# The last down-projection group's late weight tiles, and who scales, squares and sums in the final norm

## The chip, the cores and the metric

The kernel runs on one core of a Trainium2 chip. That core has five engines, each with its own instruction stream: TensorE (PE, the matmuls), VectorE (DVE), ScalarE (ACT), GpSimd (POOL) and SyncE (SP, which here only issues DMAs). They meet through semaphores. Weights and activations come from the chip's main memory by DMA into SBUF; TensorE writes its results into PSUM, from where VectorE and ScalarE evict them. The metric is the device time of one execution in microseconds (us), of which the median of a few runs counts.

## The reference

One layer of a streaming encoder for a prompt of 1024 tokens and a sample of 64: a mixer of retention and sliding-window attention, cross-attention, and a gated feed-forward part, each behind an RMS norm and added to the residual; then a final RMS norm. The change is in the last two lines of this:

```python
def rms_norm(x, g=None):
    xf = x.astype(jnp.float32)
    y = xf * lax.rsqrt(jnp.mean(xf * xf, axis=-1, keepdims=True) + EPS)
    if g is not None:
        y = y * g.astype(jnp.float32)
    return y.astype(x.dtype)

def swiglu(x, g_ffn, w_gate, w_up, w_down):
    hn = rms_norm(x, g_ffn)
    return (jax.nn.silu(hn @ w_gate) * (hn @ w_up)) @ w_down

hp = hp + swiglu(hp, g_ffn[l], w_gate[l], w_up[l], w_down[l])
...
y_prompt = rms_norm(hp, g_final)
```

The model width is 1024 and the feed-forward width 2816; everything is float32.

## The kernel before, in words

Activations are held transposed: 128 features on the partitions, 1088 tokens (prompt and sample, `T`) along the free dimension. The residual before the final norm is eight such tiles, `y[0]` to `y[7]` (`KT` = 8). In the trace and in the lists below `y[0]` goes by the name `rstd_f`, `y[1]` and `y[2]` share a tile, `y[3]` and `y[4]` another, and `y[5]`, `y[6]`, `y[7]` are tiles of their own.

Each float32 matmul is made of three: every operand is split into a high part (ScalarE's cast, L124) and a low part (VectorE's subtraction, L125), and high x high, high x low and low x high are summed in PSUM (L157 to L159 in `mm3`, L223 to L226 in `multiply`). Large products go by Strassen's scheme with seven products P1 to P7, whose weight operands are sums of raw weight tiles. In the last stages GpSimd forms these sums (L201, L202, L204, L207 in `weight_ops`).

`down` multiplies by `w_down` in three groups of the 22 blocks of 128 along the feed-forward width (8, 8 and 6). In each group the eight output rows come in pairs `m`. For each pair two raw weight tiles are loaded into a pool `wp` with two buffers for them (`raw`), split, multiplied and added to `y` (L1646, L1648). In the last group (`last`) the products P2 and P4 are left out, and `complete` squares the right half of the tokens (columns 544 to 1087, which hold the sample) as soon as its rows are done (ScalarE) and adds the squares up in `rstd` (VectorE, L1660). After that, a loop over the same row pairs loads what P2 and P4 need once more, 128x768 at a time into the same two buffers, splits it into `wb`, and hands it to `finish` in `rest`: sixteen late products of nine matmuls, for each of two quarters of the tokens (columns 0 to 271, then 272 to 543) and each of the eight rows.

`finish` runs the final norm beside these late products. It has three column ranges: 0 and 1 are the two quarters, 2 is the right half. For each range: `grow` adds the product to `y` (VectorE) and squares it (ScalarE), `gather` adds the square to `rstd` (VectorE), `sums` adds over the partitions by a matmul with ones, `roots` takes the inverse root in five small steps of VectorE and one of ScalarE, `spread` brings the roots back to all partitions by a matmul with the identity, and ScalarE copies them to `rstd` where `copied` is set. Then each row is multiplied by gain and root and stored. `scale` does it in one VectorE instruction and issues the store; `gain` (ScalarE) and `aside` (GpSimd, then the store) do it in two.

A scheduler lays out the order of each engine's instructions from the program's dependencies and its own estimates, and `queued` and `in_order` pin VectorE's and TensorE's order in `finish`. `issue_after` holds an instruction's place behind another's. Each engine then runs its list strictly in order. PSUM banks come from a pool of four pairs, taken in turn, and a product can begin only when the pair's former contents have been evicted. All loads and nearly all stores are issued by SyncE, in order.

Of the kernel before, what the change touches and what calls it, by code (L numbers as in the profile page):

```python
# [19 lines left out]
P = 128  # L20
# [89 lines left out]
class Kernel:  # L110
# [1525 lines left out]
    def down(self, starts):  # L1636
# [28 lines left out]
        for gi, g in enumerate(GROUPS):  # L1665
            last = gi == len(GROUPS) - 1
            f0, n = starts[gi], g * P // 2
            for m in range(0, KT, 2):
# [5 lines left out]
                raws = [self.wp.tile([P, 1024], F32, tag="raw", bufs=2, name="raw") for i in range(2)]  # L1674
                with self.tc.issue_after(self.loaded) if m == 2 and not last else nullcontext():
                    for i in range(2):
                        load_half(raws[i][:, :2 * n], m + i, f0, f0 + g)
                if m == KT - 4 and not last:
                    for name in ("B11", "B21" if gi == 0 else "T2"):
                        self.ahead[name, gi + 1] = list(self.fetch(name, gi + 1))  # L1680
# [10 lines left out]
                else:  # L1691
# [5 lines left out]
                    if m == 0:  # L1697
                        for name in ("B21", "T4"):
                            self.load_operand(name, gi)
                if last and m == KT - 4:  # L1700
                    nc.scalar.activation(self.root[:, 0, :1], self.rstd[:, HALF:HALF + 1], AF.Sqrt)
        rest = []
        for m in range(0, KT, 2):
            raw = self.wp.tile([P, 1024], F32, tag="raw", bufs=2, name="raw")
            for i in range(2):
                load_half(raw[:, i * n:(i + 1) * n], m + i, f0 + g // 2, f0 + g)
            ring, slots = self.slots["B11" if m < 4 else "T1"]
            q = self.rings[ring].tile("wb", slot=slots[m // 2 % 2])
            self.last_queued = self.split(raw[:, :2 * n], q[:, 0, :2 * n], q[:, 1, :2 * n])
            rest += [(m + i, q[:, :, i * n:(i + 1) * n], self.ops[("B21", "T4")[i]]) for i in range(2)]  # L1710
# [7 lines left out]
    def finish(self, y, rest):  # L1718
# [29 lines left out]
        def sums(c, *more):  # L1748
# [4 lines left out]
            for i, (a, w) in enumerate(spans):  # L1753
                for j, x in enumerate(parts):
                    self.last_mm = nc.tensor.matmul(ps[:, i, :], x[:, a:a + w], self.ones[:, :2], start=j == 0,
                                                    stop=j == len(parts) - 1).ins
# [9 lines left out]
        def spread(c, copied=True):  # L1766
            r, spans, _ = factors[c]
            for part in ((0, 2), (2, 5)) if len(spans) > 4 else ((0, len(spans)),):
# [7 lines left out]
                if copied:  # L1776
                    nc.scalar.copy(self.rstd[:, c0 + a0:c0 + a1], pb[:, :a1 - a0])
# [12 lines left out]
        def aside(c, k, queue=nc.sync):  # L1790
            o = y[k][:, cols[c]]
            nc.gpsimd.tensor_tensor(out=o, in0=o, in1=self.rstd[:, cols[c]], op=ALU.mult)
            queue.dma_start(self.io["o_y"][k, :, cols[c]], o)

        for j in range(2 * KT):
# [3 lines left out]
            if (j - 1) % KT and j:  # L1799
# [9 lines left out]
            if j == KT + 6:  # L1809
                pb0 = self.in_order(lambda: spread(0, False))[:, :HC]  # L1810
            if c and m < KT - 1:
                scale(2, m)
            if c and KT - 5 < m < KT - 1:
                gain(1, rest[m][0])
            if j == 2 * KT - 2:
                gain(2, KT - 1)
                aside(2, KT - 1)
        m = rest[-1][0]
        spare = [rest[i][0] for i in range(KT - 4, KT - 1)]
        scale(0, 0, pb0)  # L1820
        scale(0, 1, pb0)
        self.in_order(lambda: sums(1, squares[1, m]))
        roots(1, lambda: scale(0, 2, pb0))
        for k in range(3, KT):
            scale(0, k, pb0)
        pb = self.in_order(lambda: spread(1))[:, :HC]
        queues = [nc.sync, nc.scalar]
        rows = [k for k in range(KT) if k not in spare]
        for i, k in zip((2, 4, 7), spare):
            rows.insert(i, k)  # L1830
        for i, k in enumerate(rows):
# [86 lines left out]
```

## Time and profile before

| what | us |
| --- | --- |
| median of three runs | 2156.85 |
| lowest and highest of them | 2153.68, 2157.04 |
| profiled execution, its own time | 2156.32 |
| its span, first to last instruction | 2154.5 |
| TensorE busy in the span | 2133.1 |
| VectorE, ScalarE, GpSimd busy | 1550.4, 875.0, 531.9 |

The rows of the profile that the prediction shows are of four kinds. A row of a timeline gives start, duration, engine, line, operation, output and inputs, form and count, and in brackets how long the engine had been idle and what ended that. A row of waits gives total, number and longest. A row of stretches gives length, then busy time of each engine with its number of instructions, the clock granted to TensorE as a share of full, the share in which the 16 DMA engines were busy, and GB/s; where one engine alone was asked for, it is shorter. SPq and ACTq are the DMA issues of SyncE and ScalarE.

### The profile page before, as it was taken

To read this page: it belongs to the slowest core of one execution; us is meant where nothing else is said; L and a number is where in the kernel's file an instruction comes from. 1 tells how busy PE (TensorE), PEld (TensorE's weight loads), DVE (VectorE), ACT (ScalarE), POOL (GpSimd) and SP (SyncE) were. 2 spreads that over 40 slices of the span, in tenths; PEclk is the share of its full clock that TensorE was granted. 3 is DMA by queue.
4 is the path that set the end of the run, shared out by engine and by line. 5 is a ranking of instruction groups with operands and counts; after the bars stand their busy time and mean duration, and the time that the engine had idled before them with its cause. 6 is when DMAs were issued, how large, how long until landed. Compare 5 with 4: busy or idle time off the path is not lost.

```text
span 2154.5 us, 41702 instructions
## 1 busy us (share of the span) xinstructions
PE 2133.1 (99%) x16371; PEld 2082.9 (97%) x16371; DVE 1550.4 (72%) x2912; ACT 875.0 (41%) x1894; POOL 531.9 (25%) x448
## 2 busy tenths in 40 slices
PE   9999999999999999999999999999999999999997
PEld 9999999999999997889999999999999999999997
DVE  8987969776677567656545555678777777878597
ACT  8344434344434356553233343343223222344243
POOL 0000000022243125540000000015555555523531
PEclk9999999999999999999999999999999999999998
DMA  7334444434345485336443121413342232384333
GB/s 267 122 127 123 131 140 135 127 118 160 111 143 191 155 257 189 115 115 210 144 133 103 43 72 53 147 61 103 126 148 86 101 126 93 125 306 161 105 116 113
DMA packets 169893, 290.85 MB, mean 135 GB/s; under 512 B 39266, under 2 KB 96546, under 8 KB 169698
## 3 DMA queue, kind: packets, MB, share of 16 engines
q1 hardware_dynamic: 161666, 269.02, 38.8%
q0 software_dynamic: 3424, 10.82, 1.4%
q10 hardware_dynamic: 4608, 8.36, 1.0%
q8 instruction: 129, 2.11, 0.4%
q14 instruction: 66, 0.54, 0.1%
HBM read 196.97 MB, written 91.16 MB: 134 GB/s over the span
## 4 chain that ended last, share of the span: by engine, by line
PE 88%; DVE 5%; issue 2%; DMA 2%; ACT 2%; POOL 1%; SPq 0%; POOLq 0%; DVEq 0%; ACTq 0%
PE pq L226 18%; PE pq L223 17%; PE pq L224 17%; PE pd L157 8%; PE pd L158 8%; PE pd L159 8%; DVE wq L125 1%; PE pout L1078 1%; PE pss L1008 1%; PE pk L769 1%; DVE T L125 1%; PE pp L1054 1%; PE po L158 1%; PE po L159 1%; PE po L157 1%
## 5 line engine op out<-in xcount | busy, mean ns | idle before, releaser
L124 ACT CAST wq<-raw 128x512 fp32r<-128x512 f32 (+1 forms) x499 | 302.2, 614 | 560.8 <-PE pq L226 233.1
L125 DVE TENSOR_TENSOR wq<-raw,wq 128x512 fp32r<-128x512 f32 (+1 forms) x499 | 427.0, 860 | 131.9 <-ACT wq L124 128.5
L224 PE MATMUL pq<-T,wq 128*128 128x272 f32 x1832 | 492.1, 288 | 0.0
L223 PE MATMUL pq<-T,wq 128*128 128x272 f32 x1832 | 490.3, 287 | 1.4 <-ACT wq L124 0.6
L224 PE MATMUL pq<-B,wq 128*128 128x272 f32 x1592 | 426.8, 288 | 0.0
L223 PE MATMUL pq<-B,wq 128*128 128x272 f32 x1592 | 425.4, 287 | 0.0
L226 PE MATMUL pq<-T,wq 128*128 128x272 f32 x1832 | 382.7, 289 | 1.9 <-DVE wq L125 1.9
L201 POOL TENSOR_TENSOR raw<-raw 128x512 f32<-128x512 f32 (+1 forms) x44 | 64.0, 1454 | 1254.2 <-DVE wq L125 536.8
L223 PEld LDWEIGHTS pq<-T,wq 128*128 128x128 f32 x1832 | 344.3, 188 | 2.7 <-issue 1.1
L224 PEld LDWEIGHTS pq<-T,wq 128*128 128x128 f32 x1832 | 344.0, 188 | 1.0 <-issue 0.7
L226 PE MATMUL pq<-B,wq 128*128 128x272 f32 x1592 | 332.0, 289 | 0.0
L224 PEld LDWEIGHTS pq<-B,wq 128*128 128x128 f32 x1592 | 299.0, 188 | 0.5 <-issue 0.4
L223 PEld LDWEIGHTS pq<-B,wq 128*128 128x128 f32 x1592 | 298.9, 188 | 0.1
L226 PEld LDWEIGHTS pq<-T,wq 128*128 128x128 f32 x1832 | 289.6, 189 | 3.6 <-DVE wq L125 2.4
L226 PEld LDWEIGHTS pq<-B,wq 128*128 128x128 f32 x1592 | 251.7, 189 | 0.9 <-issue 0.7
L277 DVE TENSOR_TENSOR u<-pq,u 128x544 f32<-128x544 f32 x177 | 127.5, 721 | 82.4 <-PE pq L226 82.2
L616 DVE TENSOR_TENSOR stage<-pq,u 128x544 f32<-128x544 f32 x112 | 80.4, 720 | 30.3 <-PE pq L226 25.5
L157 PE MATMUL pd<-xc,wq 128*128 128x256 f32 (+1 forms) x256 | 74.6, 292 | 0.0
L159 PE MATMUL pd<-xc,wq 128*128 128x256 f32 (+1 forms) x256 | 74.3, 290 | 0.0
L158 PE MATMUL pd<-xc,wq 128*128 128x256 f32 (+1 forms) x256 | 74.1, 290 | 0.0
L1566 POOL TENSOR_TENSOR stage<-stage,rstd_f 128x544 f32<-128x544 f32 x40 | 63.8, 1605 | 39.1 <-ACT stage L1565 39.1
L204 POOL TENSOR_TENSOR raw<-raw 128x512 f32<-128x512 f32 (+1 forms) x44 | 58.9, 1339 | 51.5 <-DVE wq L125 49.0
(388 smaller groups left out, 4517.4 us busy)
## 6 DMA issues: line engine op xcount, KB each, us to landing
hl<-d_op SPq DMA_DIRECT2D x85, 272.0 KB, 5.1
d_qkv<-stage SPq DMA_DIRECT2D x44, 272.0 KB, 2.3
d_op<-stage SPq DMA_DIRECT2D x44, 272.0 KB, 2.2
d_op<-ht SPq DMA_DIRECT2D x44, 272.0 KB, 3.6
raw<-w_gate SPq DMA_DIRECT2D x22, 512.0 KB, 3.6
raw<-w_up SPq DMA_DIRECT2D x22, 512.0 KB, 5.0
raw<-w_down SPq DMA_DIRECT2D x16, 512.0 KB, 4.9
d_gate<-stage ACTq DMA_DIRECT2D x28, 272.0 KB, 2.9
```

Source lines behind the costliest of these rows:

```text
L124: self.last_cast = self.nc.scalar.copy(hi, src).ins
L125: return self.nc.vector.tensor_tensor(out=lo, in0=src, in1=hi.bitcast(F32), op=ALU.subtract).ins
L157: mm(ps, wh, xh, start=start, stop=False)
L158: mm(ps, wh, xl, start=False, stop=False)
L159: self.last_mm = mm(ps, wl, xh, start=False, stop=stop).ins
L201: tt(out=a11, in0=a11, in1=a21, op=sub)
L223: mm(ps[:, c, :HC], w[:, 0, ks], x[:, 0, cs], start=start, stop=False)
L224: mm(ps[:, c, :HC], w[:, 0, ks], x[:, 1, cs], start=False, stop=False)
L226: self.last_mm = mm(ps[:, c, :HC], w[:, 1, ks], x[:, 0, c * HC:(c + 1) * HC], start=False, stop=stop).ins
L277: add = lambda out, a, b: nc.vector.tensor_tensor(out=out, in0=a, in1=b, op=ALU.add)
L616: nc.vector.tensor_tensor(out=o, in0=ps, in1=sb, op=ALU.add)
L1566: nc.gpsimd.tensor_tensor(out=g, in0=g, in1=r[t], op=ALU.mult)
```

## The change

The diff has three parts.

First, the weights. Once the last group's first row pair has been sent off, the six extra buffers of another pool (`self.temp`) are given up, and a pool of four tiles of 128x768 is opened in their place (`raw_tile`). The last row pair's two raw tiles come from it, and so do the first two of the four late tiles (`halves`); the other two still come from `wp`. All of them are issued behind the last operand load (`self.loaded`), ahead of the last row pair's products. Second, `sums` orders its matmuls by operand rather than by token block, with one start flag for all, and the last two squares of quarter 1 go into it as operands of their own instead of being added up by VectorE first. Third, the scalings are dealt out anew: rows 5, 6 and 7 of the right half go to ScalarE's gain and GpSimd's `aside`, as does row 7 of quarter 0, for which the first quarter's roots are now copied to SBUF; of quarter 1, rows 5 and 6 go that way, no longer 4, 5 and 6.

```diff
--- before.py
+++ after.py
@@ -1671,10 +1671,17 @@
                     if last and t == 1:
                         complete(m + i, HALF, HALF)
 
-                raws = [self.wp.tile([P, 1024], F32, tag="raw", bufs=2, name="raw") for i in range(2)]
-                with self.tc.issue_after(self.loaded) if m == 2 and not last else nullcontext():
+                raws = [self.raw_tile() if last and m == KT - 2 else self.wp.tile([P, 1024], F32, tag="raw", bufs=2, name="raw")
+                        for i in range(2)]
+                with self.tc.issue_after(self.loaded) if m == (KT - 2 if last else 2) else nullcontext():
                     for i in range(2):
                         load_half(raws[i][:, :2 * n], m + i, f0, f0 + g)
+                if m == KT - 2 and last:
+                    halves = [self.raw_tile() for k in range(2)]
+                    halves += [self.wp.tile([P, 1024], F32, tag="raw", bufs=2, name="raw") for k in range(2)]
+                    with self.tc.issue_after(self.loaded):
+                        for k in range(KT):
+                            load_half(halves[k // 2][:, k % 2 * n:(k % 2 + 1) * n], k, f0 + g // 2, f0 + g)
                 if m == KT - 4 and not last:
                     for name in ("B11", "B21" if gi == 0 else "T2"):
                         self.ahead[name, gi + 1] = list(self.fetch(name, gi + 1))
@@ -1697,13 +1704,15 @@
                     if m == 0:
                         for name in ("B21", "T4"):
                             self.load_operand(name, gi)
+                        if last:
+                            self.temp.close()
+                            more = self.temp.enter_context(self.tc.tile_pool(name="halves", bufs=4, reuse_waits="tile", side="right"))
+                            self.raw_tile = lambda: more.tile([P, 768], F32, tag="raw", name="raw")
                 if last and m == KT - 4:
                     nc.scalar.activation(self.root[:, 0, :1], self.rstd[:, HALF:HALF + 1], AF.Sqrt)
         rest = []
         for m in range(0, KT, 2):
-            raw = self.wp.tile([P, 1024], F32, tag="raw", bufs=2, name="raw")
-            for i in range(2):
-                load_half(raw[:, i * n:(i + 1) * n], m + i, f0 + g // 2, f0 + g)
+            raw = halves[m // 2]
             ring, slots = self.slots["B11" if m < 4 else "T1"]
             q = self.rings[ring].tile("wb", slot=slots[m // 2 % 2])
             self.last_queued = self.split(raw[:, :2 * n], q[:, 0, :2 * n], q[:, 1, :2 * n])
@@ -1750,10 +1759,10 @@
             spans = self.spans(cols[c].stop - cols[c].start)
             ps = bank()[:, :2 * len(spans)].rearrange("p (t two) -> p t two", two=2)
             parts = [self.rstd[:, cols[c]], *more]
-            for i, (a, w) in enumerate(spans):
-                for j, x in enumerate(parts):
-                    self.last_mm = nc.tensor.matmul(ps[:, i, :], x[:, a:a + w], self.ones[:, :2], start=j == 0,
-                                                    stop=j == len(parts) - 1).ins
+            steps = [(x, i, a, w) for x in parts for i, (a, w) in enumerate(spans)]
+            for j, (x, i, a, w) in enumerate(steps):
+                self.last_mm = nc.tensor.matmul(ps[:, i, :], x[:, a:a + w], self.ones[:, :2], start=j == 0,
+                                                stop=j == len(steps) - 1).ins
             r = self.np.tile([P, 5], F32, tag="rf", bufs=2, name="rs_f")[:, :len(spans)]
             factors[c] = r, spans, ps[:, :, 0]
 
@@ -1774,7 +1783,7 @@
                                                     start=True, stop=True).ins
                 c0 = cols[c].start
                 if copied:
-                    nc.scalar.copy(self.rstd[:, c0 + a0:c0 + a1], pb[:, :a1 - a0])
+                    self.last_copy = nc.scalar.copy(self.rstd[:, c0 + a0:c0 + a1], pb[:, :a1 - a0]).ins
             return pb
 
         def scale(c, k, by=None, queue=nc.sync):
@@ -1787,16 +1796,24 @@
             o = y[k][:, cols[c]]
             nc.scalar.mul(o, o, self.gains[:, 3, k:k + 1])
 
-        def aside(c, k, queue=nc.sync):
+        def put(c, k, queue=nc.sync):
+            queue.dma_start(self.io["o_y"][k, :, cols[c]], y[k][:, cols[c]])
+
+        def aside(c, k, queue=None):
             o = y[k][:, cols[c]]
-            nc.gpsimd.tensor_tensor(out=o, in0=o, in1=self.rstd[:, cols[c]], op=ALU.mult)
-            queue.dma_start(self.io["o_y"][k, :, cols[c]], o)
-
+            with self.tc.issue_after(self.last_aside) if self.last_aside else nullcontext():
+                self.last_aside = nc.gpsimd.tensor_tensor(out=o, in0=o, in1=self.rstd[:, cols[c]], op=ALU.mult).ins
+            if queue:
+                put(c, k, queue)
+
+        self.last_aside = None
+        left = (5, 6, 7)
+        spare = (5, 6)
         for j in range(2 * KT):
             c, m = divmod(j, KT)
             ps = self.in_order(lambda: product(c, *rest[m]))
             grow(c, rest[m][0], ps)
-            if (j - 1) % KT and j:
+            if (j - 1) % KT and j and j < 2 * KT - 1:
                 gather((j - 1) // KT, rest[(j - 1) % KT][0])
             if j == 5:
                 self.in_order(lambda: sums(2))
@@ -1807,28 +1824,32 @@
                 self.in_order(lambda: sums(0))
                 roots(0)
             if j == KT + 6:
-                pb0 = self.in_order(lambda: spread(0, False))[:, :HC]
-            if c and m < KT - 1:
-                scale(2, m)
-            if c and KT - 5 < m < KT - 1:
-                gain(1, rest[m][0])
-            if j == 2 * KT - 2:
-                gain(2, KT - 1)
-                aside(2, KT - 1)
-        m = rest[-1][0]
-        spare = [rest[i][0] for i in range(KT - 4, KT - 1)]
-        scale(0, 0, pb0)
-        scale(0, 1, pb0)
-        self.in_order(lambda: sums(1, squares[1, m]))
-        roots(1, lambda: scale(0, 2, pb0))
-        for k in range(3, KT):
+                pb0 = self.in_order(lambda: spread(0))[:, :HC]
+                aside(0, KT - 1, nc.sync)
+            if c and m in (0, 1, 2, 5, 6):
+                scale(2, m if m < 3 else m - 2)
+            if c and 0 < m < 4:
+                gain(2, left[m - 1])
+            if c and m == 4:
+                gain(0, KT - 1)
+        for k in spare:
+            gain(1, k)
+        for k in range(3):
             scale(0, k, pb0)
+        for k in left:
+            aside(2, k)
+        self.in_order(lambda: sums(1, *(squares[1, rest[i][0]] for i in (KT - 2, KT - 1))))
+        roots(1, lambda: scale(0, 3, pb0))
+        for k in range(4, KT - 1):
+            scale(0, k, pb0)
+            if k < KT - 2:
+                put(2, left[k - 4])
         pb = self.in_order(lambda: spread(1))[:, :HC]
         queues = [nc.sync, nc.scalar]
-        rows = [k for k in range(KT) if k not in spare]
-        for i, k in zip((2, 4, 7), spare):
-            rows.insert(i, k)
-        for i, k in enumerate(rows):
+        for i, k in enumerate((0, 1, 2, 5, 3, 4, 6, 7)):
+            if i == 3:
+                with self.tc.issue_after(self.last_copy):
+                    put(2, left[2], nc.scalar)
             if k in spare:
                 aside(1, k, queues[i % 2])
             else:
```

VectorE, in the last group: the rows around the first weight split of the last row pair (`wq` is a split weight, `u` one of Strassen's partial sums, `pq` PSUM). Before:

```order
L125 TENSOR_TENSOR wq<-raw,wq 128x384
L1648 TENSOR_TENSOR y_22084<-u_24325,y_22084 128x544
L1646 TENSOR_TENSOR y_22085<-pq,y_22085 128x544
L1660 TENSOR_TENSOR rstd<-rstd,sq 128x544
L277 TENSOR_TENSOR u_24461<-pq,u_24460 128x544
L125 TENSOR_TENSOR wq<-raw,wq 128x384
```

And in the change:

```order
L125 TENSOR_TENSOR wq<-raw,wq 128x384 x2
L1648 TENSOR_TENSOR y_22084<-u_24329,y_22084 128x544
L1646 TENSOR_TENSOR y_22085<-pq,y_22085 128x544
L1660 TENSOR_TENSOR rstd<-rstd,sq 128x544
L277 TENSOR_TENSOR u_24465<-pq,u_24464 128x544
```

The split of the last pair's first weight, four rows further down before, now stands directly behind the last split of the pair before it (the x2).

VectorE again, around the last Strassen evictions and the first late products (`wb` is a late weight; L1737 and, in the change, L1746 add a late product to `y`). Before:

```order
L277 TENSOR_TENSOR u_24601<-pq,u_24600 128x544
L1646 TENSOR_TENSOR y_22088<-pq,y_22088 128x544
L1648 TENSOR_TENSOR y_22088<-u_24601,y_22088 128x544
L1648 TENSOR_TENSOR y_22088<-u_24602,y_22088 128x544
L125 TENSOR_TENSOR wb<-raw,wb 128x768
L1646 TENSOR_TENSOR y_22087<-pq,y_22087 128x544
L125 TENSOR_TENSOR wb<-raw,wb 128x768
L1737 TENSOR_TENSOR rstd_f<-pq,rstd_f 128x272
L1660 TENSOR_TENSOR rstd<-rstd,sq 128x544
```

And in the change:

```order
L125 TENSOR_TENSOR wb<-raw,wb 128x768
L277 TENSOR_TENSOR u_24617<-pq,u_24616 128x544
L1646 TENSOR_TENSOR y_22088<-pq,y_22088 128x544
L1646 TENSOR_TENSOR y_22087<-pq,y_22087 128x544
L1648 TENSOR_TENSOR y_22088<-u_24617,y_22088 128x544
L1648 TENSOR_TENSOR y_22088<-u_24618,y_22088 128x544
L1746 TENSOR_TENSOR rstd_f<-pq,rstd_f 128x272
L1648 TENSOR_TENSOR y_22087<-u_24618,y_22087 128x544
L1746 TENSOR_TENSOR y_22084<-pq,y_22084 128x272 x2
L1660 TENSOR_TENSOR rstd<-rstd,sq 128x544 x2
```

The last two of the four late splits stood behind and between the last evictions; all four now stand ahead of them.

GpSimd at its end, after its last weight sum (the minus rows are before, the plus rows the change; 128x544 is the right half, 128x272 a quarter):

```order
-L1792 TENSOR_TENSOR y_22088<-y_22088,rstd 128x544
-L1792 TENSOR_TENSOR y_22085<-y_22085,rstd 128x272
-L1792 TENSOR_TENSOR y_22086<-y_22086,rstd 128x272
-L1792 TENSOR_TENSOR y_22087<-y_22087,rstd 128x272
+L1805 TENSOR_TENSOR y_22088<-y_22088,rstd 128x272
+L1805 TENSOR_TENSOR y_22086<-y_22086,rstd 128x544
+L1805 TENSOR_TENSOR y_22087<-y_22087,rstd 128x544
+L1805 TENSOR_TENSOR y_22088<-y_22088,rstd 128x544
+L1805 TENSOR_TENSOR y_22086<-y_22086,rstd 128x272
+L1805 TENSOR_TENSOR y_22087<-y_22087,rstd 128x272
```

GpSimd scales six rows instead of four, three of them wide, and begins with row 7 of quarter 0 rather than with row 7 of the right half. ScalarE's gains grow by two wide rows, and its queue issues five of the last stores instead of four.

## The prediction

> **What bounds the kernel now.** I read the page first, then the table of busy time by stretch over the last 75 us, then TensorE's waits there, then the timeline of the engines named in them.
>
> ```profile
> span 2154.5 us, 41702 instructions
> PE 2133.1 (99%) x16371; PEld 2082.9 (97%) x16371; DVE 1550.4 (72%) x2912; ACT 875.0 (41%) x1894; POOL 531.9 (25%) x448
> ```
>
> TensorE is busy 99% of the span, so what can be won lies in the 21 us in which it isn't, or where it runs slowly. The change touches only the end. Two rows of the table (time, length, PE, PEld, DVE, ACT, POOL, granted clock, DMA share, GB/s) and two of the waits:
>
> ```profile
> 2090.00:2100.00 10.00, 9.38 (x73) 8.94 (x73) 10.00 (x16) 3.69 (x7) 2.78 (x2) 1.00 0.29 80
> 2120.00:2130.00 10.00, 9.68 (x66) 9.50 (x66) 8.71 (x23) 5.53 (x14) 0.00 (x0) 0.83 0.01 2
> PE pq L226 <- DVE wq L125: 0.9, 1, 0.9
> PE pq L157 <- ACT y L1788: 0.3, 1, 0.3
> ```
>
> From 2090 on TensorE has holes while VectorE is full, and in 2120 to 2130 its clock is down to 0.83 on average. The largest hole of this stretch, 1.46 us, is put down to the eviction that frees a PSUM bank; the timeline shows why that was late:
>
> ```profile
> 2117.49 0.84 ACT L124 CAST wb<-raw 128x768 fp32r<-128x768 f32 x1 [1.71 <-DMA raw<-w_down]
> 2118.36 0.96 DVE L125 TENSOR_TENSOR wb<-raw,wb 128x768 fp32r<-128x768 f32 x1
> 2119.24 0.72 DVE L1646 TENSOR_TENSOR y<-pq,y 128x544 f32<-128x544 f32 x1
> 2120.01 0.39 PE L157 MATMUL pq<-T,wb 128*128 128x272 f32 x1 [1.46 <-DVE y L1646]
> ```
>
> ScalarE's cast waits for a late weight to land, VectorE's low part waits for the cast, the eviction stands behind it in VectorE's order, and TensorE wants the bank. The 0.9 has the same root: GpSimd's weight sums for the last row pair waited 7.3 us for raw tiles.
>
> ```profile
> 2100.16 1.02 POOL L201 TENSOR_TENSOR raw<-raw 128x384 f32<-128x384 f32 x1 [7.30 <-DMA raw<-w_down]
> 2122.36 0.43 PE L157 MATMUL pq<-B,wb 128*128 128x272 f32 x1
> 2122.59 0.43 PE L158 MATMUL pq<-B,wb 128*128 128x272 f32 x1
> ```
>
> The two matmul rows show the slow spell behind the hole: starts 0.23 us apart. Elsewhere they are 0.125 apart (18 in 2.24 us, next fence). Some 15 matmuls ran so: 1.5 us lost.
>
> **Part one: weights earlier.** TensorE from P6 of the last row pair to the end of its products:
>
> ```profile
> 2104.37 0.40 PE L223 MATMUL pq<-T,wq 128*128 128x272 f32 x1
> 2112.41 0.29 PE L223 MATMUL pq<-B,wq 128*128 128x272 f32 x1
> 2114.65 0.29 PE L157 MATMUL pq<-B,wb 128*128 128x272 f32 x1
> 2128.96 1.28 PE L1773 MATMUL pq<-ident,rs_f 128*128 128x128 f32 x10
> 2129.99 0.37 PE L157 MATMUL pq<-B,wb 128*128 128x272 f32 x1
> 2140.31 0.29 PE L159 MATMUL pq<-T,wb 128*128 128x272 f32 x1
> ```
>
> A Strassen product of 18 matmuls takes 2.24 (2112.41 to 2114.65), a late product of 9 half of that, 1.12; the spread of the sample half takes 1.0 (2128.96 to 2129.99), and its sums, ten small matmuls too, as much. From 2104.37 to the ninth late product at 2129.99, without a hole, that is 4 x 2.25 + 8 x 1.12 + 2 x 1.0 = 20.0. It took 25.6: 5.6 lost, of which 2.7 are the three waits, 1.5 the slow clock, the rest slow restarts. The second eight products, 2129.99 to 2140.60, have no hole: 10.6. If weights were the only limit, the last product would end 5.6 us earlier.
>
> They are not: VectorE is next. All splits and evictions remain; they lose their waits and are done in one run. From the place to which the first split of the last pair is pulled forward, 2096.48, I add up VectorE's rows in the new order:
>
> ```profile
> 2096.48 0.72 DVE L1648 TENSOR_TENSOR y<-u,y 128x544 f32<-128x544 f32 x1
> 2099.02 0.55 DVE L125 TENSOR_TENSOR wq<-raw,wq 128x384 fp32r<-128x384 f32 x1
> 2099.48 0.72 DVE L1660 TENSOR_TENSOR rstd<-rstd,sq 128x544 f32<-128x544 f32 x1
> 2125.60 0.43 DVE L1737 TENSOR_TENSOR y<-pq,y 128x272 f32<-128x272 f32 x1
> 2127.01 0.16 DVE L1840 TENSOR_SCALAR rf_v<-pq 128x5 f32<-128x5 f32 x1
> 2128.14 0.43 DVE L1737 TENSOR_TENSOR y<-pq,y 128x272 f32<-128x272 f32 x1
> 2120.82 0.75 ACT L1788 ACTIVATE y<-y,gains 128x544 f32<-128x544 f32 x1
> 2057.49 1.30 DVE L125 TENSOR_TENSOR wq<-raw,wq 128x384 fp32r<-128x384 f32 x1
> ```
>
> Rows overlap by 0.08 (0.55 long, the next starts 0.47 on). So a wide row (0.72) costs 0.64, a 128x384 split 0.47, a 128x768 split (0.96) 0.88, a half row (0.43) 0.35, a root's steps 1.1 (2127.01 to 2128.14). From 2096.48 to the eviction of P7 there are 5 small splits, 4 large ones and 19 wide rows: 2.4 + 3.5 + 12.1 = 18.0. GpSimd's four weight sums slow VectorE where they overlap: the split at 2057.49, beside one, took 1.30 for 0.55. By that row four sums cost up to 4 x 0.75 = 3.0, at best nothing; I take the middle, 1.5. P7 is evicted at 2096.5 + 18.0 + 1.5 = 2116.0. TensorE, without a hole, wants that bank (four pairs in turn) for the third late product at 2104.37 + 4 x 2.25 + 2 x 1.12 = 2115.6: a stall of 0.4. Then come 6 wide and 3 half rows up to the last addition of the sample half's squares, 4.9: 2120.9, and ScalarE's last square, behind a gain that is new there (0.75), may cost 0.1 more: 2121.0. TensorE reaches the sums at 2116.0 + 4 x 1.12 = 2120.5: 0.5. Seven half rows and the root's steps then end at 2124.6, the seventh and eighth products at 2121.0 + 1.0 + 2.25 = 2124.3: 0.3. With the spread the ninth product starts at 2125.6, **4.4 us** earlier than 2129.99, and the last ends at 2136.2. Bounds: GpSimd costing VectorE nothing 5.6; costing 3.0, 2.9.
>
> The loads themselves I cost at nothing. The pair's 768 KB and the first two late tiles' 768 KB now go right behind the last operand loads and take 4 us at the 387 GB/s of a full queue (below), against a first need at 2096. Late tiles three and four still come from the old pool of two and go out when it is free, at about 2096.5; they are needed by 2112. If the loads were in the way, their 4 us would stand on the path.
>
> **Part two: the end.** E is the end of the last product, 2140.60 before.
>
> ```profile
> 2143.00 0.38 PE L1755 MATMUL pq<-ones,rstd 128*128 128x2 f32 x2 [2.40 <-DVE rstd L1746]
> 2144.54 0.16 DVE L1840 TENSOR_SCALAR rf_v<-pq 128x3 f32<-128x3 f32 x1 [0.77 <-PE pq L1755]
> 2147.94 0.50 DVE L1783 SCALAR_TENSOR_TENSOR rstd_f<-rstd_f,gains,pq 128x272 f32<-128x272 f32 x1
> 2147.98 2.19 POOL L1792 TENSOR_TENSOR y<-y,rstd 128x272 f32<-128x272 f32 x3 [15.86 <-ACT rstd L1777]
> 2130.75 1.38 POOL L1792 TENSOR_TENSOR y<-y,rstd 128x544 f32<-128x544 f32 x1 [25.29 <-ACT rstd L1777]
> 2133.39 0.77 DVE L1783 SCALAR_TENSOR_TENSOR y<-y,gains,rstd 128x544 f32<-128x544 f32 x1
> 2126.13 0.43 ACT L1741 ACTIVATE sq<-y 128x272 f32<-128x272 f32 x1 [0.33 <-DVE y L1737]
> ```
>
> Before, the sums waited until E+2.4 for VectorE's backlog, the root's first step came at E+3.94, the first scaling with the last root at E+7.34. Now two wide scalings (0.70 each) and one addition stand no longer ahead of the sums: VectorE has 8 evictions, 6 additions, 5 wide scalings and a root's steps in the second eight products, 2.8 + 2.1 + 3.5 + 1.1 = 9.5 against TensorE's 10.6, so it keeps up. The last eviction ends by E+0.5, ScalarE's square (0.43) by E+0.95, the last three matmuls of the sums by E+1.5; VectorE, through its next three scalings (0.42 each) by E+1.7, takes the root's first step there. From it to the first scaling it is 3.40 as before: E+5.1, **2.2 us** earlier. Six scalings instead of five end at E+7.7; GpSimd's two, 0.73 each, at E+6.6, if its four others are done: 0.73 + 3 x 1.38 from E-0.6, when the prompt's first root is copied, end at E+4.3.
>
> What ends the span is the stores, by rows of DMA share and GB/s:
>
> ```profile
> 2132.15 0.34 SPq L1793 DMA_DIRECT2D o_y<-y  x1
> 2133.00:2133.50 0.50, 1.00 0.97 387
> 2149.00:2149.50 0.50, 0.50 0.83 281
> 2152.00:2152.50 0.50, 0.50 1.01 361
> 2152.50:2153.00 0.50, 0.50 0.27 92
> ```
>
> Data ran at full share until 2152.6, E+12.0; the span closes 1.9 later. A half store (139 KB) takes 0.39 at 361 GB/s, a sample store (278 KB) 0.72 at 387, and data starts 0.85 after the issue (2132.15 to 2133.0). From E+0.2 on are issued eight half and three sample stores, 8 x 0.39 + 3 x 0.72 = 5.3, until E+6.4; then the sample store that ScalarE's queue sends behind the copy, and the last eight halves: 0.7 + 3.1, until E+10.2. That is **1.8 us** earlier, less than 2.2, so the stores are the bound here. Bounds: hidden stores 2.2; all 3.34 MB at the 281 of 2149, 11.9, until E+12.9: 0.9 lost.
>
> **Sum.** 4.4 + 1.8 = 6.2. The profiled execution took 2156.3 for its span of 2154.5; the median of the three runs is 2156.85, the lowest 2153.68. That gives 2150.1 against its own time, 2150.6 against the median; I say 2150.3.
>
> **Rivals.** *VectorE becomes the bound.* For it: it is full in 2090 to 2100, and its pauses are used up. Against it: four bank pairs take up lag. With 3.0 of slowing: 2.9 + 1.8 = 4.7 gained, 2151.8. [...]
>
> *The slow spell stays.* For it: it begins 1.7 us behind its hole, and the 0.9 us hole has none. Then 1.5 less: 2151.8. [...] Ahead of E no other place of this end shows one, so I hold to the hole.
>
> *The stores bind harder.* 0.9 lost for 1.8 won: 2153.0. For it: rates below 300 at 2149. Against it: the share was 0.83 there, so the queue was short of stores.
>
> *Slower: the clock stays at half* from the third late product on, held down by small stalls (0.4, 0.5, 0.3): 14 products x 9 matmuls x 0.10 = 12.6 lost against 6.2: 2162.7. It decides from 7 products on. Against it: the spell before lasted 3.4 us and ended in work as dense.
>
> *It doesn't do what it says:* the early loads delay the operand loads ahead of them by their 4 us, the hole only moves: 2154. Against it: one queue, served in order.
>
> **How the numbers follow.** Forecast 0.50, VectorE 0.20, slow spell 0.12, stores 0.08, loads in the way 0.06, half clock 0.04. The range 2147.8 to 2153.8 goes from the upper bounds (5.6 + 2.2 gained, and 0.7 of scatter) past the third rival and leaves out the last two and some scatter. What can be told from no change is 0.2%, 4.3 us. Faster is under 2152.5: nearly all of the forecast, most of the spell, half of VectorE as bound: 0.73. Slower than 2161.2 is the half clock alone: 0.04. The same: 0.23.
>
> **What would show it.** Right: no TensorE wait of 1 us after 2100, a full clock up to the last product, its end near 2136, the sums' wait under 1.2, store data at full share until 10 us behind it. Part one is wrong if TensorE's waits for evictions sum to over 2 us with VectorE never idle; part two if the first scaling comes by E+5.5 but the data lasts past E+11. The forecast falls if the clock is half for over 4 us ahead of E, or if ScalarE's operand casts after 2082 wait longer than before.

## The result, and the profile after

The changed kernel took 2150.59 us (median of 16 runs, 2148.19 to 2156.35), the kernel before 2156.33 (16 runs, 2152.03 to 2163.01): a ratio of 0.9976, 95% interval 0.997 to 0.9983, or 5.2 us; the two medians lie 5.7 apart. Forecast were 2150.3 and 6.2. The sum is right; its two terms are not: between the profiles shown the products gained more than their 4.4, and the end 0.6 of its 1.8. All ratios leave out two single executions that took far longer than the rest (2583 us with the weights alone, 5998 of the kernel before).

Two lines of the page after, and TensorE's two waits from 2040 on:

```profile
span 2150.0 us, 41711 instructions
PE 2130.1 (99%) x16377; PEld 2080.0 (97%) x16377; DVE 1550.7 (72%) x2909; ACT 875.7 (41%) x1897; POOL 536.5 (25%) x450
...
PE pq L1782 <- DVE rs_f L1868: 2.9, 1, 2.9
PE pq L223 <- ACT wq L124: 1.1, 2, 0.6
```

TensorE is busy 3.0 us less, for the same products. The waits of 1.46 and 0.9 for evictions and weight splits are gone; what is left lies ahead of 2095 and in the last root. The table by stretch (columns as in the prediction) shows TensorE and its clock:

```profile
2090.00:2100.00 10.00, 8.91 (x68) 8.40 (x67) 10.00 (x17) 4.43 (x10) 4.26 (x4) 1.00 0.47 160
2100.00:2110.00 10.00, 10.00 (x83) 10.00 (x82) 10.00 (x17) 5.68 (x10) 3.83 (x3) 1.00 0.06 18
2110.00:2120.00 10.00, 10.00 (x82) 10.00 (x82) 10.00 (x17) 4.96 (x9) 0.00 (x0) 1.00 0.00 1
2120.00:2130.00 10.00, 10.00 (x84) 9.90 (x83) 8.31 (x24) 5.74 (x15) 0.00 (x0) 1.00 0.03 9
```

From 2100 to 2130 TensorE has no hole and the full clock, though VectorE never rests from 2090 to 2120. TensorE's landmarks, as in the prediction: P6 of the last row pair, the first and the ninth late product, the last matmul, the sums:

```profile
2105.73 0.29 PE L223 MATMUL pq<-T,wq 128*128 128x272 f32 x1
2114.70 0.29 PE L157 MATMUL pq<-B,wb 128*128 128x272 f32 x1
2126.03 0.37 PE L157 MATMUL pq<-B,wb 128*128 128x272 f32 x1
2136.35 0.29 PE L159 MATMUL pq<-T,wb 128*128 128x272 f32 x1
2136.47 0.72 PE L1764 MATMUL pq<-ones,rstd 128*128 128x2 f32 x6
```

From P6 to the ninth late product it is 20.3 (before 25.6; 21.2 forecast). E, the end of the products, is 2136.64, and the sums follow at once. Then the root:

```profile
2136.01 5.14 POOL L1805 TENSOR_TENSOR y<-y,rstd 128x272 f32<-128x272 f32 x4 [31.61 <-DVE rstd L1755]
2138.58 0.16 DVE L1861 TENSOR_SCALAR rf_v<-pq 128x3 f32<-128x3 f32 x1 [0.24 <-PE pq L1764]
...
2139.26 0.63 DVE L1866 TENSOR_TENSOR rf_t<-rs_f 128x3 f32<-128x3 f32 x1
2139.93 1.25 DVE L1867 SCALAR_TENSOR_TENSOR rf_t<-rf_t,rf_v 128x3 f32<-128x3 f32 x1
2141.22 0.16 DVE L1868 SCALAR_TENSOR_TENSOR rs_f<-rf_t,rs_f 128x3 f32<-128x3 f32 x1
2143.54 0.50 DVE L1792 SCALAR_TENSOR_TENSOR rstd_f<-rstd_f,gains,pq 128x272 f32<-128x272 f32 x1 [0.94 <-ACT rstd L1786]
```

The first step stands at E+1.94 (E+1.7 forecast, E+3.94 before). But two steps over three columns last 0.63 and 1.25. Before, they were

```profile
2145.22 0.16 DVE L1845 TENSOR_TENSOR rf_t<-rs_f 128x3 f32<-128x3 f32 x1
2145.42 0.16 DVE L1846 SCALAR_TENSOR_TENSOR rf_t<-rf_t,rf_v 128x3 f32<-128x3 f32 x1
```

Each now ends only after one of GpSimd's multiplies has. GpSimd makes four in 5.14, from 2136.01 to 2141.15; the third ends at 2139.88 and the fourth at 2141.15, VectorE's two steps at 2139.89 and 2141.18. From the first step to the first scaling it is 4.96, where the forecast kept the 3.40 of before. The stores, by stretches:

```profile
2138.00:2138.50 0.50, 0.50 (x5) 0.45 (x5) 0.34 (x1) 0.00 (x0) 0.50 (x1) 1.00 0.69 235
...
2142.50:2143.00 0.50, 0.50 (x3) 0.29 (x2) 0.10 (x1) 0.00 (x0) 0.00 (x0) 0.50 0.79 255
...
2147.50:2148.00 0.50, 0.00 (x0) 0.00 (x0) 0.00 (x0) 0.00 (x0) 0.00 (x0) 0.50 0.98 361
2148.00:2148.50 0.50, 0.00 (x0) 0.00 (x0) 0.00 (x0) 0.00 (x0) 0.00 (x0) 0.50 0.16 52
```

Data flows from E+1.5 (the share of 0.69 in the first stretch) and ends at 2148.1, E+11.4: E+10.2 was forecast, and it was E+12.05 before.

### The profile page after: what moved, and what is told of

Same layout as the page of the kernel before. It is cut to its first block, busy times and chain, and to the rows that moved or that the text cites. A ratio compares the mean times of both kernels' runs of the same rounds, so it can differ in the third digit from the quotient of the medians.

```text
span 2150.0 us, 41711 instructions
## 1 busy us (share of the span) xinstructions
PE 2130.1 (99%) x16377; PEld 2080.0 (97%) x16377; DVE 1550.7 (72%) x2909; ACT 875.7 (41%) x1897; POOL 536.5 (25%) x450
```

## The experiments

Two theories stood against each other for the end. **The lock:** VectorE's steps with both inputs in SBUF stand still while GpSimd multiplies a wide row. **The stores:** the bytes that leave behind E set the end, whatever the root does. The table gives, for each profiled run, five stretches in us, read from timelines as above (the data's end from the share of the last stretch of 0.5): P6 of the last pair to the ninth late product; from there to E; E to the root's first step; first step to first scaling; E to the end of the data. The last column is the way from P6 to the end of the data. It leaves out what differs from run to run ahead of this place: P6 of the second row pair alone begins anywhere from 2078.1 to 2083.0, which is more than the experiments move.

| run | P6 to ninth | to E | E to root | root to scaling | E to data end | all |
| --- | --- | --- | --- | --- | --- | --- |
| before | 25.62 | 10.61 | 3.94 | 3.40 | 12.05 | 48.3 |
| before, again | 24.00 | 10.61 | 5.15 | 3.40 | 13.26 | 47.9 |
| changed | 20.30 | 10.61 | 1.94 | 4.96 | 11.44 | 42.4 |
| changed, again | 20.29 | 10.61 | 1.94 | 4.95 | 11.43 | 42.3 |
| weights alone | 20.29 | 10.61 | 4.84 | 3.40 | 12.94 | 43.8 |
| norm alone | 24.45 | 10.61 | 1.93 | 4.95 | 11.42 | 46.5 |
| wide multiplies first | 20.30 | 11.40 | 4.16 | 3.40 | 12.09 | 43.8 |
| wide multiplies short | 20.29 | 10.60 | 1.94 | 3.39 | 11.03 | 41.9 |
| loads first | 20.31 | 10.61 | 1.93 | 4.97 | 11.43 | 42.4 |
| root in PSUM | 20.30 | 10.61 | 1.94 | 2.70 | 10.98 | 41.9 |
| wide multiplies held | 20.29 | 10.61 | 1.94 | 2.70 | 10.99 | 41.9 |
| root in PSUM, one early | 20.28 | 10.61 | 2.51 | 3.41 | 10.45 | 41.3 |
| root in PSUM, two early | 20.28 | 10.68 | 4.17 | 3.41 | 12.12 | 43.1 |

### Each part alone

All diffs are against the changed kernel. Weights alone: `finish` is that of the kernel before. Norm alone: `down` is.

```diff
-        for k in spare:
-            gain(1, k)
...
+        self.in_order(lambda: sums(1, squares[1, m]))
+        roots(1, lambda: scale(0, 2, pb0))
...
```

> The early weights alone; the norm as it was before. If the two parts add up, this has the changed kernel's products: TensorE without a hole of over 0.7 us after 2100, no half-clock spell, the ninth late product some 4.2 us earlier than before (5.0 behind P6 of the last row pair), and the tail of before: sums late, the root's first step near E+3.9, first scaling near E+7.3, span end near E+13.9. Span near 2150.3, time 4 us under before. Rival: the gain in the products needs the new dealing out of VectorE's work in the second eight products; then E gains 3 at most and the time is 3 us under before or less.

```diff
-            raw = halves[m // 2]
+            raw = self.wp.tile([P, 1024], F32, tag="raw", bufs=2, name="raw")
+            for i in range(2):
+                load_half(raw[:, i * n:(i + 1) * n], m + i, f0 + g // 2, f0 + g)
...
```

> The norm dealt out anew alone; the late weights as before. Theory of the lock (VectorE's root steps that read two operands from SBUF stand still while GpSimd multiplies a wide row): the same 5 us from the root's first step to the first scaling as in the changed kernel against 3.4 before, the tail 0.3 to 0.6 us shorter than the 13.9 of before, the hole of 1.4 us and the half-clock spell behind it still there; time 0 to 1 us under before. Rival (what the tail lost in the changed kernel comes from the early loads' shift of the work): the first scaling comes at E+5.1 and the time is 1.8 us under before.

Weights alone: 2151.54 (11 runs; ratio to before 0.9986, 0.9977 to 0.9995). Norm alone: 2153.26 (11 runs; 0.9999, 0.999 to 1.0009). The products' gain needs nothing of the new norm: 20.29 either way. The root of the weights alone came at E+4.84, not at the E+3.9 expected: the clock granted to TensorE fell to half at E+2.7, on the sums ahead of it. The norm alone shows the long root (4.95) with the late weights as before, so the early loads have no part in it. The two parts together, 4.2 and 1.6 on the way from P6 against the mean of the two profiles of before, make up the changed kernel's 5.7; their times (3.0 and 0.2 with intervals of 2 on either side) do not contradict that.

One thing was not expected. The norm alone has a hole where the kernel before has one, of 1.27 for 1.46, but no slow spell behind it:

```profile
2117.57 0.39 PE L157 MATMUL pq<-T,wb 128*128 128x272 f32 x1 [1.27 <-DVE y L1646]
2117.80 0.29 PE L158 MATMUL pq<-T,wb 128*128 128x272 f32 x1
2117.92 0.29 PE L159 MATMUL pq<-T,wb 128*128 128x272 f32 x1
```

### Before and after, profiled once more

> The kernel before, profiled once more. If the half-clock spell at 2121.7 belongs to the hole of 1.46 ahead of it (the forecast), it is there again: 15 matmuls some 0.1 apart more, 35.9 to 36.3 us from P6 of the last row pair to the end of the products. If it was chance, as the run with the norm alone suggests (a hole of 1.27 and no spell, 35.1), there is none and the products take about 35.0.

> The changed kernel, profiled once more. If the second hole of 0.45 at 2093 is the early loads' doing, it is there again; if chance, there is one hole of 0.4 to 0.6 as in the other runs with the early loads. From P6 of the last pair to the ninth late product 20.3 again; first step of the root to first scaling 5.0 if the spread falls under the half clock, 4.3 if not.

Before, again:

```profile
2118.69 0.39 PE L157 MATMUL pq<-T,wb 128*128 128x272 f32 x1 [1.13 <-DVE y L1646]
2118.92 0.29 PE L158 MATMUL pq<-T,wb 128*128 128x272 f32 x1
2119.05 0.29 PE L159 MATMUL pq<-T,wb 128*128 128x272 f32 x1
...
2140.77 0.58 PE L1755 MATMUL pq<-ones,rstd 128*128 128x2 f32 x2 [2.40 <-DVE rstd L1746]
2143.52 0.16 DVE L1840 TENSOR_SCALAR rf_v<-pq 128x3 f32<-128x3 f32 x1 [1.99 <-PE pq L1755]
```

Starts 0.125 apart behind a hole of 1.13: no slow spell, and 24.0 to the ninth product, not 25.6. These single executions took 2155.33 and, for the changed kernel, 2151.5. So the half clock of the first profile does not come with every hole at this place. A hole as long as 1.46 was not seen again, so whether its length decides is not shown. Here the half clock falls elsewhere: the sums of the last quarter run in pairs of 0.57 (0.36 to 0.38 in the first profile), and the root's first step comes 1.2 later. The changed kernel's second hole at 2093 is not fixed either: this time there is one, of 0.44, and all five stretches are the same to 0.01.

### The loads ahead of the operands

```diff
-                    with self.tc.issue_after(self.loaded):
+                    with self.tc.issue_after(self.last_low):
...
```

The place of the last pair's two raw loads is changed in the same way. `last_low` is an instruction of VectorE, so it does not hold SyncE's loads back, and they go out ahead of the last three operand loads (`hl`):

```profile
2067.05 15.60 SPq L118 DMA_DIRECT2D raw<-w_down  x10
2082.70 1.38 SPq L118 DMA_DIRECT2D hl<-d_op  x3
```

> The changed kernel with the last pair's two raw loads and the first four late pieces issued ahead of the last three operand loads instead of right behind them. If loads in the way cost their transfer, as the prediction's bound says: the last operand's casts wait some 4 us longer, TensorE's hole near 2092 grows from 0.6 to about 4, and the end comes 3 to 4 us later than in the changed kernel. Rival (the queue has slack there, so that loads ahead of the operands cost nothing either): the hole stays under 1 and the time is that of the changed kernel.

2150.65 (9 runs; 0.998, 0.997 to 0.9989): the rival of the expectation holds. Table by stretch of this run, then of the changed kernel:

```profile
2074.00:2078.00 4.00, 4.00 (x35) 4.00 (x34) 4.00 (x6) 0.52 (x1) 2.85 (x3) 1.00 1.00 344
```

```profile
2074.00:2078.00 4.00, 4.00 (x34) 4.00 (x33) 4.00 (x6) 0.52 (x1) 2.40 (x2) 1.00 0.06 19
2086.00:2090.00 4.00, 4.00 (x34) 4.00 (x33) 2.33 (x4) 1.62 (x4) 2.03 (x2) 1.00 1.00 350
```

The loads do take 4 us at full share, but from 2074 to 2078, where the changed kernel's queue moved next to nothing (19 GB/s) ahead of its next raw loads. So the run shows that there is room on both sides of the operand loads; what they would cost if they stood in their way was not shown. That they cost nothing beyond the scatter where the change puts them is shown by the stretch ahead, P6 of the second row pair to P6 of the last: 23.6 and 23.7 before, 23.3 to 24.2 in the ten profiles with early weights, 23.6 with the norm alone.

### Is it the lock?

> The changed kernel, but GpSimd's three wide multiplies cover 16 of their 544 columns only; the scaling of the other 528 columns of these three row tiles is left out, the stores are whole. Theory of the lock: from the root's first step to the first scaling 3.4 (5.0 in the changed kernel), first scaling near E+5.4, span some 1.5 us shorter. Rival (the root's steps are slow because of what VectorE and ScalarE themselves have queued there): 5.0 as before, the second and third of the root's steps last over 0.5 us as in the changed kernel.

```diff
-            o = y[k][:, cols[c]]
+            w = slice(cols[c].start, cols[c].start + 16) if c == 2 else cols[c]
+            o = y[k][:, w]
...
```

2148.6 (10 runs; 0.9972, 0.9962 to 0.9981). GpSimd's four multiplies take 1.81 instead of 5.14 and are done before the root:

```profile
2131.84 1.81 POOL L1806 TENSOR_TENSOR y<-y,rstd 128x272 f32<-128x272 f32 x4 [31.59 <-DVE rstd L1755]
2135.08 0.16 DVE L1867 TENSOR_TENSOR rf_t<-rs_f 128x3 f32<-128x3 f32 x1
2135.28 0.16 DVE L1868 SCALAR_TENSOR_TENSOR rf_t<-rf_t,rf_v 128x3 f32<-128x3 f32 x1
```

The root is back at 3.39, so GpSimd's multiplies are the cause. But the data still ends at E+11.03. Whether two SBUF inputs matter, or any work beside GpSimd, the next run tells:

```diff
+            if c == 1:
+                room = bank()
+                v, t = room[:, :len(spans)], room[:, 16:16 + len(spans)]
...
+            q(lambda: stt(t, out, -0.5, v, ALU.mult, ALU.mult))
+            q(lambda: nc.vector.tensor_tensor(out=t, in0=t, in1=out, op=ALU.mult))
...
```

> The changed kernel with the last root's correction written so that none of VectorE's steps has two inputs in SBUF: the variance and the product stand in PSUM, and the order of the two multiplications is turned. GpSimd's wide multiplies stay beside it. Theory of the lock by two SBUF inputs: the steps last 0.16 to 0.2 each beside a running GpSimd multiply (0.63 and 1.25 in the changed kernel), first step to first scaling 3.4 to 3.6, first scaling near E+5.4; the stores bind then, data end near E+11.0 as in the run with short multiplies, so only 0.4 us off the span. Rival (GpSimd's multiply stops any VectorE instruction of this size that reads SBUF at all): 5.0 as before.

2149.38 (5 runs; 0.9967, 0.9955 to 0.9979).

```profile
2132.66 6.78 POOL L1808 TENSOR_TENSOR y<-y,rstd 128x272 f32<-128x272 f32 x6 [31.62 <-DVE rstd L1755]
2135.91 0.17 DVE L1870 SCALAR_TENSOR_TENSOR pq<-rs_f,pq 128x3 f32<-128x3 f32 x1
2136.11 0.17 DVE L1871 TENSOR_TENSOR pq<-pq,rs_f 128x3 f32<-128x3 f32 x1
2136.31 0.16 DVE L1875 SCALAR_TENSOR_TENSOR rs_f<-pq,rs_f 128x3 f32<-128x3 f32 x1
```

GpSimd multiplies all through these steps, and with one input in PSUM they take 0.16 to 0.17. The lock is one of two SBUF inputs: beside a GpSimd multiply the longer step took 1.25 with two, 0.17 with one. (First scaling comes 2.70 behind the first step, not 3.40, since the spread here still ran at the full clock: 0.93 for 1.65.)

> The changed kernel with GpSimd's second and third wide multiply held, by a small GpSimd operation that reads the root, until the last root's steps are done. Theory of the lock: first step to first scaling 3.4, first scaling near E+5.4; the held multiplies end near E+8.2 and their stores leave late, so that the data ends between E+11.0 and E+11.5. Rival (the stores are all that counts): the later wide stores move the data's end past E+11.5.

```diff
-        for k in left:
-            aside(2, k)
+        aside(2, left[0])
...
+        with self.tc.issue_after(self.last_aside):
+            self.last_aside = nc.gpsimd.tensor_scalar(held[:, :1], factors[1][0][:, :1], 1.0, None, ALU.mult).ins
+        for k in left[1:]:
+            aside(2, k)
```

2148.43 (12 runs; 0.9971, 0.9962 to 0.998). The root is free of the lock again, the wide stores leave late, and the data ends at E+10.99 as in the two runs above. Three ways to be rid of the lock, one end: behind the lock, worth 0.45, the stores bind.

### Fewer bytes behind the last product

> The changed kernel with GpSimd's three wide multiplies put ahead of its narrow one, in the second eight products instead of beside the last root. Theory of the lock: from the root's first step to the first scaling 3.4 again (5.0 in the changed kernel), first scaling near E+5.4; three of the 278 KB stores leave some 5 us earlier, so the data ends with the last half stores near E+10; span 1.5 us under the changed kernel. The price by the same theory: VectorE's half additions of two SBUF operands (0.43 each) stand behind the wide multiplies in the products, by at most 3 x 1.25; if its backlog at the last product grows by over 1.5 the gain is eaten. Rival (the stores are the bound whatever the root does): 0.7 us or less under the changed kernel, the data at full share to the end.

```diff
             if c and m == 4:
                 gain(0, KT - 1)
+                for k in left:
+                    aside(2, k)
...
-        for k in left:
-            aside(2, k)
```

2150.33 (11 runs; 0.9981, 0.9972 to 0.999): no gain over the changed kernel. From the root's first step to the first scaling it is 3.40, as the theory of the lock has it, but the lock has moved into the products:

```profile
2126.06 1.88 DVE L1792 SCALAR_TENSOR_TENSOR rstd_f<-rstd_f,gains,rstd 128x544 f32<-128x544 f32 x1
...
2128.22 1.51 DVE L1792 SCALAR_TENSOR_TENSOR y<-y,gains,rstd 128x544 f32<-128x544 f32 x1
```

Two wide scalings of 0.78 take 1.88 and 1.51, VectorE is behind to the end, E comes 0.8 later and the root 2.2 later relative to E. Of these 2.2, 0.6 is the clock and not the lock: it fell to half at E+2.5, and the last six matmuls of the sums took 1.44, for 0.83 in the run below. That VectorE's backlog could eat the gain was named ahead, and it did; the shorter time expected did not come.

> The run with the root's steps in PSUM, and also the first of GpSimd's three wide multiplies in the second eight products. If the data end is set by the bytes that leave behind the last product, 278 KB fewer take 0.75 us off: data end near E+10.3, the first scaling still near E+5.5. VectorE's slack there is 1.1 by the prediction's sum, so one multiply (1.2 to 1.4 of lock) fits, where three did not. Rival (one multiply already puts VectorE behind): the last eviction and the sums come 0.5 or more later relative to E and eat the gain.

```diff
                 gain(0, KT - 1)
+                aside(2, left[0])
...
-        for k in left:
+        for k in left[1:]:
```

The steps of the root stand in PSUM as in the run with the root in PSUM.

2148.12 (5 runs; 0.9964, 0.9952 to 0.9975), the best of all by its median, though its interval overlaps that of the changed kernel; on the way from P6 it is 1.0 shorter. One early multiply meets VectorE where it has slack, and the data ends 0.5 earlier than with the root in PSUM alone, for 278 KB less (0.75 was expected). GpSimd's narrow multiply now begins 0.1 ahead of VectorE's last wide scaling, which takes 1.30 for 0.78, and the sums wait 0.41 for the square behind it:

```profile
2124.15 1.37 POOL L1808 TENSOR_TENSOR y<-y,rstd 128x544 f32<-128x544 f32 x1 [22.38 <-ACT rstd L1789]
2133.38 3.88 POOL L1808 TENSOR_TENSOR y<-y,rstd 128x272 f32<-128x272 f32 x3 [7.86 <-ACT rstd L1789]
2133.48 1.30 DVE L1795 SCALAR_TENSOR_TENSOR y<-y,gains,rstd 128x544 f32<-128x544 f32 x1
```

> The run with the root in PSUM and one early wide multiply, and a second wide multiply early. If the bytes behind the last product set the data's end: another 278 KB fewer, data end near E+9.8. If VectorE's slack of 1.1 is the limit: two multiplies lock out up to 2.5 of its two-SBUF rows, the last eviction comes 1 or more behind that of the run with one, and the time is the same or longer.

The diff is the same line for `left[1]`. 2151.59 (11 runs; 0.9979, 0.997 to 0.9988): two are too many.

```profile
2129.60 1.90 DVE L1795 SCALAR_TENSOR_TENSOR rstd_f<-rstd_f,gains,rstd 128x544 f32<-128x544 f32 x1
2140.62 1.44 PE L1764 MATMUL pq<-ones,sq 128*128 128x2 f32 x6 [0.52 <-ACT sq L1750]
```

A wide scaling takes 1.90 beside them, the root starts at E+4.17 and the gain is eaten. Here too 0.6 of the later root is the half clock on the last six matmuls (1.44 for 0.83). Without it, by an estimate from the table's 12.12 and 10.45, the data would still end 1.1 later than with one. VectorE's slack holds one.

## Why the prediction was right, and where it was not

**The slow waits and their root: right.** With the early weights no run has a hole of over 0.2 from P6 to the last product.

**VectorE as the next limit: wrong in size.** The step that failed is "four sums cost up to 4 x 0.75 = 3.0, at best nothing; I take the middle, 1.5". Counted from P6, VectorE's work starts where the forecast has it (its first split of the last pair at 2097.84, 7.89 ahead of P6, as the 2096.48 before). Then GpSimd cost it some 0.4:

```profile
2098.47 1.44 POOL L201 TENSOR_TENSOR raw<-raw 128x384 f32<-128x384 f32 x1 [4.25 <-DVE wq L125]
2099.58 0.91 DVE L1660 TENSOR_TENSOR rstd<-rstd,sq 128x544 f32<-128x544 f32 x1
2100.41 0.71 DVE L277 TENSOR_TENSOR u<-pq,u 128x544 f32<-128x544 f32 x1
2101.04 0.74 DVE L125 TENSOR_TENSOR wq<-raw,wq 128x384 fp32r<-128x384 f32 x1
```

An addition and a split, both of two SBUF inputs, take 0.2 longer each (0.72 and 0.55 else); the evictions, which read PSUM, take their 0.71. GpSimd gave way instead: 1.44 for 1.02. So no stall came, and 20.3 is the 20.0 of the sum without holes plus slow restarts. The first rival (VectorE as the bound) falls in every run with the early weights: the way to the ninth product is 20.28 to 20.31. The chances put half of this rival above 2152.5, past its 2151.8; no run shows a slowing of these sums past the 3.0 behind that figure, and here it was 0.4.

**The slow clock: counted as certain, which it is not.** "So I hold to the hole": with holes of 1.13 and 1.27 at the same place no spell came in two of three profiles. The 1.5 counted as won belongs to one execution. Against the second profile of before, part one won 24.0 - 20.3 = 3.7; against the first, 5.3; the forecast of 4.4 lies between because its two errors, 1.2 of stalls that did not come and 1.5 of a spell that need not be there, nearly cancel. Between the profiles first compared 5.3 and 0.6 make 5.9, close to the 6.2 with neither term right: that the forecast came within 0.3 us of the measured median is in part luck. The rival that let the spell stay was right in so far as hole and spell need not come together here; but no half clock stood ahead of E in any profile with the early weights. Whether the length of the holes decides stays open (see the last section).

**Sums at once, root at E+1.7: right** (E+1.94).

**"From it to the first scaling it is 3.40 as before": wrong.** It took 4.96. This is the step of the forecast that failed. The change puts GpSimd's wide multiplies beside the root, and two of the root's steps have both inputs in SBUF. The prediction counted VectorE's slowing beside GpSimd (1.30 for 0.55) for the weight sums, where it came to some 0.4, and not for the root, where these two steps took 0.63 and 1.25 for 0.16 each. The same lock held GpSimd's narrow multiply beside VectorE's wide scaling, which began 0.1 ahead of it (1.28, not 0.73), and with it the first store behind E. The long root costs some 0.45 at the end of the data, by three runs.

**The stores as the bound: right, but 0.8 too cheap.** Without the lock they end at E+11.0, not 10.2: data starts at E+1.5 instead of 1.05, and 3.34 MB then take 9.5 us, 352 GB/s, where the terms of the sum (0.39 and 0.72 a store) allow 9.1. The rival that made them bind harder had the place, but not the size: by it the data ends at E+12.9.

**The end together:** 0.6 won in the profiles first compared. Against the second profile of before it is 1.8, since there the half clock caught the sums behind their wait of 2.40; in the changed kernel the sums do not wait, and in both of its profiles they were done (the root's first step at E+1.94) when the clock fell, at E+4.1 and E+3.8.

**Loads at nothing: right.** The loads landed in the order of their issue: in the changed kernel the last three operand loads, issued from 2083.1 to 2084.1, landed 5.4, 5.6 and 5.8 later (5.1, 5.4 and 5.6 before), the first raw load behind them, issued at 2084.6, 6.3 later. **The half clock from the third late product on:** in no profile.

## What to carry to other kernels

When work is dealt to GpSimd, list what VectorE does at that moment, and by its operands: rows with both inputs in SBUF were held up beside it here (a wide scaling took 1.90 for 0.78), and even a step of 0.16 on the critical path became 1.25; with one operand in PSUM such steps took 0.17. A slow spell in one profile is worth a second profile of the same kernel before it goes into a sum. Where the bytes behind the last product set the end, measure each way of making room against the slack of the engine that it loads: here one row fitted, two cost more than they brought.

## What the runs showed of the hardware that was not expected

The clock granted to TensorE fell to half at no fixed distance from the end of the work: in the profile of before 5.2 us behind the last product, in its second profile some 2.2, in the run with the weights alone 2.7, in the changed kernel 4.1. Where it fell ahead of the sums, a pair of these took 0.57, for 0.36 at the full clock; where it fell only when the spread was done or nearly done, the spread took 0.93 to 0.96, for 1.65 at half. The first moved the last root of the kernel before by 1.2 us between its two profiles, the second the first scaling by 0.7 between runs without the lock.

In the profile of before, from 2060 on, the granted clock changed three times. The rows give the length, TensorE's busy time, the granted clock, the DMA share and GB/s:

```profile
2121.90:2122.10 0.20, 0.20 (x2) 0.54 0.00 0
2125.20:2125.40 0.20, 0.20 (x3) 0.68 0.00 0
2145.80:2146.00 0.20, 0.17 (x1) 0.52 0.12 38
```

By the mean of each stretch it fell at 2121.92, rose 3.41 later, at 2125.33, and fell again at 2145.81. In the 3.41 ahead of the first fall TensorE waited twice, 1.46 and 0.31, 1.77 in all. At the same place it waited 1.27 and 0.23 with the norm alone, and once, 1.13, in the second profile of before, and no spell followed. So the length of the waits may decide, and not chance alone. This is an estimate from three profiles; no run varied the hole by itself.
